# Squares of x summed by TensorE, inverse roots and half-wise scaling on GpSimd, and another order of fill and banks in the second block of a two-block transformer kernel

## The chip, the core and the metric

The kernel runs on one core of a Trainium2 chip. The engines are TensorE (PE, with its weight loads PEld), VectorE (DVE), ScalarE (ACT), GpSimd (POOL) and SyncE (SP, which issues most of the DMAs). Each engine works through its own list of instructions in order, and waits at an instruction until what that one needs is there. The metric is the device time of one execution in microseconds (us).

## The reference

Two transformer blocks run one after the other on 512 tokens of width 1024, all in float32. Cut to what matters:

```python
# first block
xn = rms_norm(x, norm_gain)            # x * rsqrt(mean(x*x, -1) + EPS) * gain
qa, ka, va, za, qi, ki, wi, qb, kb, vb, zb = split(xn @ w_in)
qa, ka, qb, kb = (rms_norm(t_per_head, its_gain) for each of the four)   # 8 heads of 64
score = sum over 4 index heads of relu(qi . ki) * wi        # causal
a_out = attention(qa, ka, va) over the 128 best keys of each token by score
b_out = dilated attention(qb, kb, vb)
x = x + concat(a_out * silu(za), b_out * silu(zb)) @ w_out
# second block
h = rms_norm(x, norm_mix)
q, (kc, vc, ks, vs, kw, vw), g_attn, u_pool, g_merge = split(h @ w_in_2)
a = (gated sum of attention on compressed, selected and windowed keys) @ w_branch_attn
b = pool_mixer(u_pool) @ w_branch_pool     # running means over 2, 4, 8, 16 tokens
x = x + (sigmoid(ga) * a + sigmoid(gb) * b) @ w_out_2
x = x + square(relu(rms_norm(x, norm_mlp) @ w_ff1)) @ w_ff2
return rms_norm(x, norm_final)
```

## The kernel before

**Products.** Every matrix product is made of three matmuls on rounded operands. A weight unit is a DMA into `wr` (or `wx`), a rounded high part `wh` (ACT, or a CAST on DVE) and a remainder `wl` (POOL as two instructions of 512 columns, or DVE as one of 1024). x is held as `XH` and `XL` in the same way, eight parts of 128 features by 512 tokens, named `xh_69` and following. The sum is wh*xh + wl*xh + wh*xl. Two `wr` tiles and three each of `wh` and `wl` take turns, so a unit's DMA waits for a remainder two units earlier. PSUM has 8 banks, by tag: three `g`, two `s`, two `pt`, one `av`. A GEMM that puts tokens on partitions (`steps_t`) takes one bank for each of four token blocks, from the tags in its argument `tags`; one that puts features there (`steps_e`) takes two `g` banks.

**Start.** Ten matmuls on a tile of zeros come first. The index GEMM (queries, keys and weights of the index heads, 324 columns) then runs in four units of two x parts each, with banks `s, s, pt, av`, and both `wh` and `wl` by DVE. `load_x` is its hook: for each part it makes `XH` (ACT), `XL` (DVE) and the squares (ACT), and POOL adds the squares of the eight parts into `ssum` (tile `th`). After the last unit `tok_stats([ssum])` sums `ssum` over the features by four matmuls of 128 x 1 against ones, and DVE makes the inverse root `rs_t`.

**First block.** The weight GEMMs run through x without its norm, and the norm is applied when a bank is read. `qk_pair(s, p)` makes queries and keys of two heads for branch b (s = "b") or a: GEMM into `raw`, squares and sums per head (`qm`), inverse roots by `rsqrt` (`qy`, with `qt` as scratch) by nine short instructions on DVE after one integer one, and one multiplication of all of `raw` by `qy`, by POOL for branch b and by DVE for branch a. PE then transposes `raw` (`pt<-ident,raw`), and ACT and DVE make the operands `qs`, `kh`, `kl`. `select` finds the 128 best keys on DVE with rounds of MAX8 and MATCH_REPLACE8, from about 69 to 162 us. The tiles `pth` and `ptl` are the two parts of transposed probabilities, `sb` the probabilities before.

**Order on the engines.** A tile scheduler sets the order outside the attention stretches. Inside them `weave` sets it by hand: it takes steps of the attention in turn and puts fill GEMMs between them, from a list that it works through in order. In the second block the first such list is taken with `prepare()`, which makes compressed keys and values; its pieces are `values_t` (values, 280 columns with the gates), `raw_t("q0")` (queries of group 0), and `pool_in(0)`, `pool_in(1)`, whose banks `evac_u` reads with DVE and then adds shifted copies on POOL, one addition for window 2 up to four for window 16 (tile `th`). `stack_group(0, ...)` transposes queries into `qs`, and `compressed(0)` uses them with compressed keys `kch`, `kcl` in a bank `s`.

Of the kernel before, what the change touches and what calls it, by code (L numbers as in the profile page):

```python
# [13 lines left out]
AF = mybir.ActivationFunctionType  # L14
OP = mybir.AluOpType
# [4 lines left out]
S = 512  # L20
# [123 lines left out]
def _program(ctx, tc, nc, ap, units, out, out1):  # L144
# [7 lines left out]
    def bank(tag):  # L152
        return ps.tile([128, 512], F32, name=tag, tag=tag, bufs={"g": 3, "s": 2, "pt": 2, "av": 1}[tag])

    def mm(o, lhsT, rhs, start, stop):
        nc.tensor.matmul(o, lhsT, rhs, start=start, stop=stop, skip_group_check=True)  # L156
# [4 lines left out]
    def act(o, i, f=AF.Copy, **kw):  # L161
        nc.scalar.activation(o, i, f, **kw)  # L162

    def stt(o, a, s, b, op0, op1, eng=None):
        (eng or nc.vector).scalar_tensor_tensor(o, a, s, b, op0=op0, op1=op1)

    def tt(o, a, b, op, eng=None):
        (eng or nc.vector).tensor_tensor(o, a, b, op=op)  # L168

    def ts(o, a, s1, s2=None, op0=OP.mult, op1=None, eng=None):  # L170
        if op1 is None:
            (eng or nc.vector).tensor_scalar(o, a, s1, None, op0=op0)
        else:
            (eng or nc.vector).tensor_scalar(o, a, s1, s2, op0=op0, op1=op1)
# [32 lines left out]
    def run(steps):  # L207
        for _ in steps:
            pass
# [7 lines left out]
    def steps_t(name, us, XH, XL, evac, tbs=range(NB), tags=("g",) * 4, hook=None, last=None, **conv):  # L217


        n = us[0][3]  # L220
        per = 512 // n if n <= 256 else 1
        tbs = list(tbs)
        groups = [tbs[q:q + per] for q in range(0, len(tbs), per)]
        banks = [bank(tags[q]) for q in range(len(groups))]
        at = lambda q, r: banks[q][:, r * n:(r + 1) * n]
        for iu, u in enumerate(us):
            then = hook and hook(u)
            k0, kk, wh, wl = wload(name, u, **conv)
            if then:
                then()  # L230
            for q, group in enumerate(groups):
                for k in range(kk):
                    for r, t in enumerate(group):
                        st = iu == 0 and k == 0 and r == 0
                        en = iu == len(us) - 1 and k == kk - 1
                        xh = XH[k0 + k][:, t * 128:(t + 1) * 128]
                        xl = XL[k0 + k][:, t * 128:(t + 1) * 128]
                        mm(at(q, r), xh, wh[:, k, :], st, False)
                        mm(at(q, r), xh, wl[:, k, :], False, False)
                        mm(at(q, r), xl, wh[:, k, :], False, en)  # L240
                    yield 3 * n * len(group)
        if last:
            last()
        for q, group in enumerate(groups):
            rest = [evac(t, at(q, r)) for r, t in enumerate(group)]
            for then in rest:
                if callable(then):
                    then()
# [18 lines left out]
        for c in range(nch):  # L267
            evac(c, banks[c])

    def rsqrt(y, m, tmp):  # L270

        ts(y.bitcast(I32), m.bitcast(I32), -0.5, 1597463007.0, OP.mult, OP.add)
        for _ in range(3):
            stt(tmp, y, -0.5, y, OP.mult, OP.mult)
            tt(tmp, tmp, m, OP.mult)
            stt(y, tmp, 1.5, y, OP.add, OP.mult)

    def weave(main, slots, fills, total):

        chain = itertools.chain(*fills)  # L280
        done = 0
        with tc.manual_schedule(engines={mybir.EngineType.PE}):
            for i in range(slots):
                next(main)
                while done < total * (i + 1) / slots:
                    c = next(chain, None)
                    if c is None:
                        break
                    done += c
            run(chain)  # L290
# [7 lines left out]
    def tok_stats(*args):  # L298
        run(tok_stats_steps(*args))

    def tok_stats_steps(parts, blocks=range(NB)):


        n = len(blocks)
        cols = slice(blocks[0], blocks[-1] + 1)
        b = bank("pt")
        for part in parts:
            for i in range(n):
                mm(b[:, i:i + 1], part[:, i * 128:(i + 1) * 128], ones, part is parts[0] and i == 0, part is parts[-1])
        m = consts.tile([128, NB], F32, name="st_m", tag="st_m")[:, :n]  # L310
        tmp = consts.tile([128, NB], F32, name="st_t", tag="st_t")[:, :n]
        y = rs_t[:, cols]
        ts(m, b[:, :n], 1.0 / D, EPS, OP.mult, OP.add)
        rsqrt(y, m, tmp)
        yield
        b = bank("pt")
        for i in range(n):
            tr(b[:, i * 128:(i + 1) * 128], y[:, i:i + 1].to_broadcast([128, 128]))
        act(rs_b[:, cols.start * 128:cols.stop * 128], b[:, :n * 128])
        yield b  # L320
# [16 lines left out]
    def T(shape, dt=F32, tag=None, bufs=1):  # L337
        return sb.tile(shape, dt, name=tag, tag=tag, bufs=bufs)

    ssum = T([128, S], tag="th")  # L340


    zero = T([128, S], F32, tag="nbm", bufs=2)
    nc.vector.memset(zero, 0.0)
# [1 line left out]
    b = bank("g")  # L346
    for _ in range(10):
        mm(b, z16[:, :128], z16[:, :512], True, True)

    def load_x(unit):  # L350
        ks = range(unit[1], unit[1] + unit[2])
        raw = {k: T([128, S], tag="mix", bufs=5) for k in ks}
        for k in ks:
            nc.sync.dma_start(raw[k], ap["xT"][:, k, :])

        def parts():
            for k, xr in raw.items():
                act(XH[k], xr, scale=ng[:, k:k + 1])
                stt(XL[k], xr, ng[:, k:k + 1], view(XH[k]), OP.mult, OP.subtract)
                if k == 0:  # L360
                    act(ssum, xr, AF.Square)
                else:
                    sq = T([128, S], tag="z", bufs=3)
                    act(sq, xr, AF.Square)
                    tt(ssum, ssum, sq, OP.add, nc.gpsimd)

        return parts

# [156 lines left out]
    def evac_idx(tb, o):  # L525
# [1 line left out]
        ts(wi[:, tb, :], idx[:, tb, 320:324], 1.0 / 16)  # L527

    gemm_t("w1", units["w1"]["idx"], XH, XL, evac_idx, hook=load_x, tags=("s", "s", "pt", "av"),
           last=lambda: tok_stats([ssum]), hi="dve", lo="dve")  # L530
    cstrip = cload("strip", [128, S], eng=nc.sync)
    gcol = cload("gcol", [128, 4], eng=nc.sync)
    gq = consts.tile([128, 2], F32, name="gq")
# [15 lines left out]
    for i in range(1, NB):  # L549
        n = (i + 1) * 128  # L550
        score[i] = T([128, n], tag=f"sel{i}")
        for h in range(4):
            b = scores(QI[h // 2][:, h % 2, i * 128:(i + 1) * 128], KIH[:, 0], KIL[:, 0], i)
            r = T([128, S], tag="sb", bufs=3)
            act(r[:, :n], b[:, :n], AF.Relu)
            prev = score[i]
            if h == 0:
                prev = T([128, S], tag="nbm", bufs=2)[:, :n]
                ts(prev, cstrip[:, (3 - i) * 128:(3 - i) * 128 + n], -1.0, eng=nc.gpsimd)
            stt(score[i], r[:, :n], wi[:, i, h:h + 1], prev, OP.mult, OP.add)  # L560

    def select(i):

# [13 lines left out]
    ML = [T([128, S], F32R, tag=f"ml{c}") for c in range(8)]  # L577
    QK, VX, Z, RAW = {}, {}, {}, {}

    def qk_pair(s, p):  # L580
        raw = T([128, NB, 4, 64], tag="raw", bufs=2)
        yield from steps_t("w1", units["w1"][f"qk{s}{p}"], XH, XL,
               lambda tb, o: act(raw[:, tb].rearrange("p h d -> p (h d)"), o, scale=rs_t[:, tb:tb + 1]))
        m = T([128, NB * 4], tag="qm", bufs=2)
        for t in range(0, NB, 2):
            sq = T([128, 2, 4, 64], tag="th")
            act(sq, raw[:, t:t + 2], AF.Square)
            nc.vector.reduce_sum(m[:, 4 * t:4 * t + 8], sq.rearrange("p b h d -> p (b h) d"), axis=AX.X)
        ts(m, m, 1.0 / 64, EPS, OP.mult, OP.add)
        y = T([128, NB * 4], tag="qy", bufs=2)  # L590
        tmp = T([128, NB * 4], tag="qt", bufs=2)
        rsqrt(y, m, tmp)
        f = raw.rearrange("p b h d -> p (b h) d")
        tt(f, f, y[:, :, None].to_broadcast([128, NB * 4, 64]), OP.mult, nc.gpsimd if s == "b" else None)
        RAW[s, p] = raw

    def stack_pair_q(s, p):
# [106 lines left out]
            for hl in range(2):  # L704
                yield pair_job(n, hl, hooks)

    run(qk_pair("b", 0))
    run(qk_pair("b", 1))
    stack_pair_q("b", 0)
    stack_pair_k("b", 0)  # L710
# [191 lines left out]
        ts(gates[:, tb], o[:, 256:280], r)  # L902

    def values_t():
        yield from steps_t("w2", units["w2"]["vv"], XH, XL, evac_v, tags=("g", "g", "g", "s"))
        act(gates, gates, AF.Tanh, scale=0.5)
        ts(gates, gates, 0.5, 0.5, OP.mult, OP.add)

# [134 lines left out]
    def pool_in(p):  # L1043
        yield from steps_e("w2", units["w2"][f"u{p}"], XH, XL, evac_u(p))
# [31 lines left out]
            yield  # L1076

    run(raw_t("kk"))
    weave(prepare(), len(order), [values_t(), raw_t("q0"), pool_in(0), pool_in(1)], 4.15 * task)
    PTH, PTL = prob_tiles(T)  # L1080
    cmp = [compressed(0), compressed(1)]
    hooks = {
# [214 lines left out]
```

## Time and profile before

| | |
|---|---|
| time, median of 3 runs | 1064.28 us (1060.01 to 1065.57) |
| the profiled execution | 1063.42 us, of which the span from first to last instruction is 1061.3 us |
| PE busy in the span | 1030.1 us, 97% |
| DVE, ACT, POOL busy | 620.3, 549.8, 318.3 us |
| mean granted TensorE clock | 0.990 of full speed |

The profile is of one execution: engine by engine, what ran when, and where an engine stood idle, which semaphore it then waited for. Times are from the span's start. A matmul's duration includes its passage through the array, and matmuls overlap, so the distance between the starts of two is what the next one costs. "[2.92 <-DVE ptl L168]" says that the engine had been idle for 2.92 us and was released by the instruction of line 168 on DVE that writes `ptl`. The 2.1 us outside the span belong to each execution.

### The profile page before, as it was taken

What the parts mean: (1) busy time and instruction counts of PE and PEld (TensorE: products, weight loads), DVE (VectorE), ACT (ScalarE), POOL (GpSimd) and SP (SyncE); (2) the same over time, 40 slices, a digit from 0 to 9 for tenths busy, and PEclk for the clock granted to TensorE, in tenths of its full rate; (3) what the DMA queues carried; (4) which work ended last, traced back from release to release, by engine and by line L of the source; (5) the groups of instructions that cost most, each with busy time, mean ns of one, the idle gap of its engine ahead of it and who ended that gap; (6) DMA issues with size and microseconds to landing.
All of it is one profiled execution on the core that took longest, in us unless ns stands there. A gap on an engine that the chain in (4) does not pass through costs nothing.

```text
span 1061.3 us, 15516 instructions
## 1 busy us (share of the span) xinstructions
PE 1030.1 (97%) x5675; PEld 886.7 (84%) x5675; DVE 620.3 (58%) x1388; ACT 549.8 (52%) x1041; POOL 318.3 (30%) x280
## 2 busy tenths in 40 slices
PE   7999999999999999899999999999999999999996
PEld 5998988999888897787888888888888888888886
DVE  6589998766757755867867323545442234443333
ACT  4557676787765354678788433434331123443321
POOL 5543442455645337522222467400000000000001
PEclk8999999999999999999999999999999999999999
DMA  5334433444567364111111223522222223222212
GB/s 186 107 96 139 117 107 100 137 125 124 164 204 233 125 200 139 60 40 41 61 53 48 70 90 114 184 80 99 100 99 88 91 99 100 99 99 87 92 60 80
DMA packets 41835, 115.07 MB, mean 108 GB/s; under 512 B 5904, under 2 KB 7312, under 8 KB 41760
## 3 DMA queue, kind: packets, MB, share of 16 engines
q1 hardware_dynamic: 41568, 113.96, 33.4%
q8 instruction: 45, 0.74, 0.3%
q14 instruction: 30, 0.25, 0.1%
q0 software_dynamic: 192, 0.12, 0.1%
HBM read 97.90 MB, written 6.33 MB: 98 GB/s over the span
## 4 chain that ended last, share of the span: by engine, by line
PE 78%; DVE 13%; ACT 3%; DMA 2%; issue 2%; POOL 1%; SPq 1%; DVEq 0%; ACTq 0%; POOLq 0%
PE g L156 66%; PE s L156 4%; PE av L156 4%; PE pt L159 4%; DVE sel L568 1%; DVE m L567 1%; DVE ptl L168 1%; DMA wx<-in_w_dram 1%; DVE sb L399 1%; ACT wh L162 1%; POOL wl L168 1%; DVE mix L168 1%; DVE raw L168 1%; PE pt L156 1%; DMA mix<-in_xT_dram 1%
## 5 line engine op out<-in xcount | busy, mean ns | idle before, releaser
L168 POOL TENSOR_TENSOR wl<-wr,wh 128x512 fp32r<-128x512 f32 (+1 forms) x148 | 194.5, 1335 | 233.9 <-ACT wh L162 220.7
L162 ACT ACTIVATE wh<-wr 128x1024 fp32r<-128x1024 f32 (+1 forms) x124 | 130.3, 1052 | 171.8 <-PE g L156 141.8
L156 PE MATMUL g<-wh,xh 128*128 128x256 f32 (+1 forms) x504 | 147.2, 292 | 1.1 <-ACT raw L162 1.1
L156 PE MATMUL g<-wl,xh 128*128 128x256 f32 (+1 forms) x504 | 143.8, 285 | 1.9 <-POOL wl L168 1.9
L156 PE MATMUL g<-wh,xl 128*128 128x256 f32 (+1 forms) x504 | 143.2, 284 | 0.0
L168 DVE TENSOR_TENSOR wl<-wr,wh 128x1024 fp32r<-128x1024 f32 (+1 forms) x54 | 66.7, 1235 | 102.5 <-ACT wh L162 102.4
L156 PE MATMUL g<-xh,wh 128*128 128x512 f32 x304 | 125.2, 413 | 0.0
L156 PE MATMUL g<-xh,wl 128*128 128x512 f32 x304 | 119.8, 395 | 0.0
L156 PE MATMUL g<-xl,wh 128*128 128x512 f32 x304 | 119.7, 394 | 0.0
L168 POOL TENSOR_TENSOR res<-res,rs_b 128x256 f32<-128x256 f32 x6 | 4.2, 732 | 366.2 <-ACT rs_b L162 366.2
L156 PE MATMUL g<-hh,wl 128*128 128x512 f32 (+1 forms) x272 | 103.4, 380 | 0.0
L156 PE MATMUL g<-hl,wh 128*128 128x512 f32 (+1 forms) x272 | 103.0, 379 | 0.0
L156 PE MATMUL g<-hh,wh 128*128 128x512 f32 (+1 forms) x272 | 102.2, 376 | 0.0
L156 PE MATMUL g<-yh,wl 128*128 128x512 f32 x256 | 100.9, 394 | 0.0
L156 PE MATMUL g<-yl,wh 128*128 128x512 f32 x256 | 100.3, 392 | 0.0
L156 PE MATMUL g<-yh,wh 128*128 128x512 f32 x256 | 99.7, 389 | 0.0
L156 PEld LDWEIGHTS g<-wl,xh 128*128 128x128 f32 x504 | 96.4, 191 | 3.7 <-POOL wl L168 2.3
L156 PEld LDWEIGHTS g<-wh,xh 128*128 128x128 f32 x504 | 96.3, 191 | 2.4 <-ACT raw L162 1.3
L156 PEld LDWEIGHTS g<-wh,xl 128*128 128x128 f32 x504 | 96.3, 191 | 0.7 <-issue 0.5
L162 ACT ACTIVATE sb<-sb,mx 128x512 f32<-128x512 f32 (+3 forms) x128 | 71.5, 559 | 33.7 <-DVE mx L399 32.4
L162 ACT ACTIVATE sb<-sb,ri 128x512 f32<-128x512 f32 (+3 forms) x128 | 70.8, 558 | 34.2 <-DVE ri L404 25.8
L162 ACT ACTIVATE wh<-wx 128x1024 fp32r<-128x1024 f32 x35 | 37.1, 1060 | 86.1 <-PE g L156 73.3
(275 smaller groups left out, 2263.0 us busy)
## 6 DMA issues: line engine op xcount, KB each, us to landing
wr<-in_w_dram SPq DMA_DIRECT2D x48, 512.0 KB, 3.7
wr<-in_wf_dram SPq DMA_DIRECT2D x43, 512.0 KB, 3.2
wx<-in_wf_dram SPq DMA_DIRECT2D x21, 512.0 KB, 3.2
wr<-in_wo_dram SPq DMA_DIRECT2D x15, 512.0 KB, 3.6
wx<-in_w_dram SPq DMA_DIRECT2D x12, 512.0 KB, 3.2
mix<-in_xT_dram SPq DMA_DIRECT2D x16, 256.0 KB, 3.9
strip<-vec_dram SPq DMA_DIRECT2D x16, 256.0 KB, 3.3
x_dram<-mix SPq DMA_DIRECT2D x16, 256.0 KB, 3.5
```

Source lines behind the costliest of these rows:

```text
L156: nc.tensor.matmul(o, lhsT, rhs, start=start, stop=stop, skip_group_check=True)
L159: nc.tensor.transpose(o, in_, ident[:n, :n])
L162: nc.scalar.activation(o, i, f, **kw)
L168: (eng or nc.vector).tensor_tensor(o, a, b, op=op)
L399: nc.vector.tensor_tensor_reduce(out=p[:, :n], in0=b[:, :n], in1=nbm, scale=1.0, scalar=3e38, op0=OP.add, op1=OP.min, accum_out=mx)
L567: nc.vector.max(out=m8, in_=w)
L568: nc.vector.match_replace(out=w, in_to_replace=m8, in_values=w, imm_value=-3e38)
```

## The change

1. `x_stats`, a generator that `load_x` feeds, sums the squares of each part on TensorE: four matmuls 128 x 1 against ones per part into one bank `pt`, 32 in all in place of 4. The tile `ssum` and POOL's seven additions are gone; the inverse root follows the eighth part.
2. The first score term of `select`'s input uses the mask strip itself with a subtraction; three POOL instructions (`nbm<-strip`) are gone.
3. `rsqrt` can run its three rounds on another engine. All qk pairs but (b, 0) run them on POOL, four instructions of 128 x 16 a round, 12 in place of DVE's 9; the integer step stays on DVE. The multiplication of `raw` is made in two halves, queries first. For (b, 0) the `wl` and the scaling are now on DVE.
4. In the second block the list of fill pieces begins with `pool_in(1)`, and `values_t` uses banks `g, s, g, g` in place of `g, g, g, s`.

```diff
+    def rsqrt(y, m, tmp, eng=None):
         ts(y.bitcast(I32), m.bitcast(I32), -0.5, 1597463007.0, OP.mult, OP.add)
+        if eng:
+            for _ in range(3):
+                tt(tmp, y, y, OP.mult, eng)
+                tt(tmp, tmp, m, OP.mult, eng)
+                ts(tmp, tmp, -0.5, 1.5, OP.mult, OP.add, eng)
+                tt(y, y, tmp, OP.mult, eng)
+            return
         for _ in range(3):
             stt(tmp, y, -0.5, y, OP.mult, OP.mult)
...
-    ssum = T([128, S], tag="th")
...
+    def x_stats():
+        b = bank("pt")
+        while True:
+            part, k = yield
+            for i in range(NB):
+                mm(b[:, i:i + 1], part[:, i * 128:(i + 1) * 128], ones, k == i == 0, k == KD - 1)
+            if k == KD - 1:
+                run(tok_stats_steps(None, bank_done=b))
...
-                if k == 0:
-                    act(ssum, xr, AF.Square)
-                else:
-                    sq = T([128, S], tag="z", bufs=3)
-                    act(sq, xr, AF.Square)
-                    tt(ssum, ssum, sq, OP.add, nc.gpsimd)
+                sq = T([128, S], tag="z", bufs=3)
+                act(sq, xr, AF.Square)
+                stats.send((sq, k))
...
     gemm_t("w1", units["w1"]["idx"], XH, XL, evac_idx, hook=load_x, tags=("s", "s", "pt", "av"),
-           last=lambda: tok_stats([ssum]), hi="dve", lo="dve")
+           hi="dve", lo="dve")
...
             if h == 0:
-                prev = T([128, S], tag="nbm", bufs=2)[:, :n]
-                ts(prev, cstrip[:, (3 - i) * 128:(3 - i) * 128 + n], -1.0, eng=nc.gpsimd)
-            stt(score[i], r[:, :n], wi[:, i, h:h + 1], prev, OP.mult, OP.add)
+                stt(score[i], r[:, :n], wi[:, i, h:h + 1], cstrip[:, (3 - i) * 128:(3 - i) * 128 + n],
+                    OP.mult, OP.subtract)
...
-        rsqrt(y, m, tmp)
-        f = raw.rearrange("p b h d -> p (b h) d")
-        tt(f, f, y[:, :, None].to_broadcast([128, NB * 4, 64]), OP.mult, nc.gpsimd if s == "b" else None)
+        pool = nc.gpsimd if (s, p) != ("b", 0) else None
+        rsqrt(y, m, tmp, pool)
+        y = y.rearrange("p (b h) -> p b h", h=4)
+        for x in (slice(0, 2), slice(2, 4)):
+            tt(raw[:, :, x], raw[:, :, x], y[:, :, x, None].to_broadcast([128, NB, 2, 64]), OP.mult,
+               pool if s == "b" else None)
...
-    run(qk_pair("b", 0))
+    run(qk_pair("b", 0, "dve"))
...
-        yield from steps_t("w2", units["w2"]["vv"], XH, XL, evac_v, tags=("g", "g", "g", "s"))
+        yield from steps_t("w2", units["w2"]["vv"], XH, XL, evac_v, tags=("g", "s", "g", "g"))
...
-    weave(prepare(), len(order), [values_t(), raw_t("q0"), pool_in(0), pool_in(1)], 4.15 * task)
+    weave(prepare(), len(order), [pool_in(1), values_t(), raw_t("q0"), pool_in(0)], 4.15 * task)
```

**PE at the start.** The last of the ten matmuls on zeros (`g<-nbm`) and the first rows of the index GEMM, before:

```order
L156 MATMUL g<-nbm 128x512
L156 MATMUL s<-wh,xh_69 128x324 x2
L156 MATMUL pt<-wh,xh_69 128x324
L156 MATMUL av<-wh,xh_69 128x324
L156 MATMUL s<-wl,xh_69 128x324
```

and after:

```order
L156 MATMUL g<-nbm 128x512
L156 MATMUL pt<-ones,z 128x1 x8
L156 MATMUL s<-wh,xh_69 128x324 x2
L156 MATMUL pt<-wh,xh_69 128x324
L156 MATMUL av<-wh,xh_69 128x324
L156 MATMUL s<-wl,xh_69 128x324
```

Eight matmuls on the squares (`z`) of two parts now stand ahead of the unit's GEMM, and eight more ahead of each later unit; the four on the summed squares behind the last unit are gone.

**POOL in the first block.** Remainders of weights (`wl`) and the scaling of the second to fourth pair of branch b, before:

```order
L168 TENSOR_TENSOR wl<-wr,wh 128x512 x3
L168 TENSOR_TENSOR raw<-raw,qy 128x1024
L168 TENSOR_TENSOR wl<-wr,wh 128x512 x7
L168 TENSOR_TENSOR raw<-raw,qy 128x1024
L168 TENSOR_TENSOR wl<-wr,wh 128x512 x8
L168 TENSOR_TENSOR raw<-raw,qy 128x1024
```

and after, from the remainders ahead of the second pair's scaling on:

```order
L168 TENSOR_TENSOR wl<-wr,wh 128x512 x10
L168 TENSOR_TENSOR qt<-qy 128x16
L168 TENSOR_TENSOR qt<-qt,qm 128x16
L174 TENSOR_SCALAR qt<-qt 128x16
L168 TENSOR_TENSOR qy<-qy,qt 128x16
L168 TENSOR_TENSOR qt<-qy 128x16
L168 TENSOR_TENSOR qt<-qt,qm 128x16
L174 TENSOR_SCALAR qt<-qt 128x16
L168 TENSOR_TENSOR qy<-qy,qt 128x16
L168 TENSOR_TENSOR qt<-qy 128x16
L168 TENSOR_TENSOR qt<-qt,qm 128x16
L174 TENSOR_SCALAR qt<-qt 128x16
```

The twelfth short row (`qy<-qy,qt`), the two halves of `raw` and six rows of `wl` follow. The short rows stand where before one long multiplication stood, with the weights' remainders of later units queued behind them.

**ACT in the second block.** Queries of group 0 (`qs`), the pooled branch's input (`mh` with a number) and compressed values (`vc`), before:

```order
L162 ACTIVATE mh_5212<-th 128x512
L162 ACTIVATE qs<-pt 64x512 x2
L162 ACTIVATE wh<-wr 128x1024
L162 ACTIVATE qs<-pt 64x512 x2
L162 ACTIVATE mh_5229<-th 128x512
```

and after:

```order
L162 ACTIVATE wh<-wr 128x1024
L162 ACTIVATE qs<-pt 64x512 x2
L162 ACTIVATE wh<-wr 128x1024
L162 ACTIVATE qs<-pt 64x512 x2
L162 ACTIVATE vc<-pt,half 128x2x64 x4
L162 ACTIVATE wh<-wx 128x1024
L162 ACTIVATE mh_5401<-th 128x512
```

Both query rows now stand ahead of the `mh` of `pool_in(0)`; the `mh` rows of `pool_in(1)` have moved further up, ahead of the compressed keys.

## Rows read from the trace of the kernel before

**Rows 1.** The page, part 1: busy us, share of the span, instructions.

```profile
PE 1030.1 (97%) x5675; PEld 886.7 (84%) x5675; DVE 620.3 (58%) x1388; ACT 549.8 (52%) x1041; POOL 318.3 (30%) x280
```

**Rows 2.** What PE waited for, whole span: total us, times, longest.

```profile
PE s L156 <- DVE wh L197: 3.9, 3, 2.0
PE pt L159 <- DVE ptl L168: 3.4, 2, 2.9
...
PE s L156 <- DVE qs L165: 1.9, 1, 1.9
...
PE av L156 <- ACT pch L162: 1.5, 1, 1.5
```

**Rows 3.** Busy time by stretch; granted clock, DMA share, GB/s last.

```profile
77.00:165.00 88.00, 82.96 (x586) 76.91 (x585) 85.40 (x257) 57.98 (x129) 35.52 (x27) 0.98 0.42 120
...
365.00:375.00 10.00, 7.49 (x46) 7.03 (x46) 5.63 (x9) 5.20 (x9) 4.11 (x4) 0.83 0.34 91
...
418.00:430.00 12.00, 9.96 (x43) 7.75 (x42) 10.05 (x14) 4.66 (x8) 7.60 (x11) 0.86 0.26 87
430.00:500.00 70.00, 65.36 (x384) 55.81 (x383) 51.92 (x165) 55.40 (x130) 24.09 (x25) 1.00 0.13 46
```

**Rows 4.** Timeline of PE at the start: start, duration, instruction.

```profile
1.50 4.45 PE L156 MATMUL g<-nbm 128*128 128x512 bf16 x10 [1.50 <-DVE nbm L344]
...
27.45 0.31 PE L156 MATMUL s<-wl,xh 128*128 128x324 f32 x1
...
27.60 0.31 PE L156 MATMUL s<-wh,xl 128*128 128x324 f32 x1
...
30.41 0.95 PE L156 MATMUL pt<-ones,th 128*128 128x1 f32 x8
...
31.21 0.36 PE L156 MATMUL g<-wh,xh 128*128 128x256 f32 x1
```

**Rows 5.** Timeline of POOL and DVE at the start.

```profile
14.13 4.80 POOL L168 TENSOR_TENSOR th<-th,z 128x512 f32<-128x512 f32 x3
...
17.74 1.55 DVE L197 CAST wh<-wr 128x648 fp32r<-128x648 f32 x1
...
21.70 0.48 DVE L197 CAST wh<-wr 128x648 fp32r<-128x648 f32 x1
```

**Rows 6.** Busy time and granted clock of short stretches after PE stood idle.

```profile
21.17:26.73 5.56, 5.56 (x20) 5.56 (x21) 2.42 (x4) 1.06 (x1) 0.90 (x1) 0.50 0.58 190
160.47:163.49 3.02, 3.02 (x8) 2.45 (x9) 2.20 (x10) 1.05 (x2) 0.00 (x0) 0.50 0.54 130
...
422.00:426.00 4.00, 3.84 (x12) 2.96 (x13) 3.87 (x6) 1.55 (x3) 3.35 (x4) 0.62 0.06 25
```

**Rows 7.** Groups of DVE instructions between 77 and 160 us.

```profile
L165 DVE SCALAR_TENSOR_TENSOR qt<-qy 128x16 f32<-128x16 f32 x7 | 3.1, 438 | 0.0
...
L168 DVE TENSOR_TENSOR qt<-qt,qm 128x16 f32<-128x16 f32 x7 | 2.7, 390 | 0.0
...
L165 DVE SCALAR_TENSOR_TENSOR qy<-qt,qy 128x16 f32<-128x16 f32 x7 | 2.6, 376 | 0.0
...
L174 DVE TENSOR_SCALAR qm<-qm 128x16 f32<-128x16 f32 x2 | 0.3, 166 | 0.0
```

**Rows 8.** Groups of POOL instructions by shape, whole span.

```profile
L168 POOL TENSOR_TENSOR nbm<-strip,sel 128x512 f32<-128x512 f32 x8 | 10.4, 1296 | 6.4 <-DVE mx L399 5.0 <-DMA strip<-vec_dram 1.4
...
L168 POOL TENSOR_TENSOR nbm<-strip,sel 128x256 f32<-128x256 f32 x8 | 6.7, 842 | 7.3 <-DVE qt L165 4.1 <-DVE mx L399 3.2
...
L1011 POOL MEMSET th<- 128x16 f32 x10 | 1.1, 111 | 4.6 <-DVE ml L168 3.4 <-DVE th L168 1.0
```

**Rows 9.** Timeline at the third pair's scaling.

```profile
110.79 1.91 POOL L168 TENSOR_TENSOR raw<-raw,qy 128x1024 f32<-128x1024 f32 x1 [2.07 <-DVE qy L165]
...
112.84 0.60 PE L159 MATMUL pt<-ident,raw 128*128 128x128 f32 x4
```

**Rows 10.** Timeline of ACT at group 0's queries, second block.

```profile
419.56 0.63 ACT L162 ACTIVATE mh<-th 128x512 fp32r<-128x512 f32 x1 [3.13 <-DVE th L168]
```

More of the change, by code (lines that the diff above doesn't have):

```diff
@@ L268, in steps_e @@
             evac(c, banks[c])
-    def rsqrt(y, m, tmp):
+    def rsqrt(y, m, tmp, eng=None):
         ts(y.bitcast(I32), m.bitcast(I32), -0.5, 1597463007.0, OP.mult, OP.add)
+        if eng:
[5 more added lines that the diff above has]
+            return
         for _ in range(3):
@@ L299, in tok_stats, with tok_stats_steps @@
         run(tok_stats_steps(*args))
-    def tok_stats_steps(parts, blocks=range(NB)):
+    def tok_stats_steps(parts, blocks=range(NB), bank_done=None):
         n = len(blocks)
         cols = slice(blocks[0], blocks[-1] + 1)
-        b = bank("pt")
-        for part in parts:
+        b = bank_done or bank("pt")
+        for part in parts or ():
             for i in range(n):
@@ L348, in _program @@
         mm(b, z16[:, :128], z16[:, :512], True, True)
+    def x_stats():
[6 more added lines that the diff above has]
+                run(tok_stats_steps(None, bank_done=b))
+    stats = x_stats()
+    next(stats)
     def load_x(unit):
@@ L555, in _program @@
             act(r[:, :n], b[:, :n], AF.Relu)
-            prev = score[i]
             if h == 0:
-                prev = T([128, S], tag="nbm", bufs=2)[:, :n]
-                ts(prev, cstrip[:, (3 - i) * 128:(3 - i) * 128 + n], -1.0, eng=nc.gpsimd)
-            stt(score[i], r[:, :n], wi[:, i, h:h + 1], prev, OP.mult, OP.add)
+                stt(score[i], r[:, :n], wi[:, i, h:h + 1], cstrip[:, (3 - i) * 128:(3 - i) * 128 + n],
+                    OP.mult, OP.subtract)
+            else:
+                stt(score[i], r[:, :n], wi[:, i, h:h + 1], score[i], OP.mult, OP.add)
     def select(i):
@@ L578, in _program, with qk_pair @@
     QK, VX, Z, RAW = {}, {}, {}, {}
-    def qk_pair(s, p):
+    def qk_pair(s, p, lo="pool"):
         raw = T([128, NB, 4, 64], tag="raw", bufs=2)
         yield from steps_t("w1", units["w1"][f"qk{s}{p}"], XH, XL,
-               lambda tb, o: act(raw[:, tb].rearrange("p h d -> p (h d)"), o, scale=rs_t[:, tb:tb + 1]))
+               lambda tb, o: act(raw[:, tb].rearrange("p h d -> p (h d)"), o, scale=rs_t[:, tb:tb + 1]), lo=lo)
         m = T([128, NB * 4], tag="qm", bufs=2)
```

## The prediction

> **What bounds the kernel now.** The page comes first, and in it the busy time of the engines: PE works 1030.1 of 1061.3 us [rows 1], so only two things can shorten the kernel: less work on PE, or fewer of the 31 us in which it stands idle. The change adds matmuls, so its gain can lie in the idle time alone. The waits of PE say what released it [rows 2]: nearly all releases come from DVE, in three kinds: weights at the start (`wh`, 3.9 us), transposed probabilities (`ptl` 3.4), queries (`qs` 1.9). The table of stretches then says where [rows 3]: 5.0 us idle in 77 to 165, where DVE is busy 85.4 of 88 us; 2.5 us in 365 to 375; 2.0 in 418 to 430; 4.6 in 430 to 500. A stall costs more than its length: in short stretches behind idle time the granted clock is 0.50 (the 1.2 GHz level) or near it [rows 6]. So I add to each stall what the slow stretch behind it loses, its length times one minus the granted clock.
>
> The sum is made on the profiled 1063.42 us, 2.1 of which lie outside the span. That is 0.86 under the median of the runs, so the result is raised by as much.
>
> **Squares on TensorE.** Added: 28 matmuls of 128 x 1. The trace has four of them as eight records in 30.41 to 31.21, so 0.20 us each [rows 4], and 32 cost 6.4 us, 5.6 more than now. Removed: nothing that PE did, but seven POOL additions, three of which fill 4.80 us from 14.13 [rows 5], and POOL's three strip instructions. What they did is seen on DVE: the CAST of a weight unit took 1.55 us beside one and 0.48 alone [rows 5], and PE waited 3.9 us for `wh` [rows 2]. After the last wait 5.56 us passed at 0.50, so 2.8 were lost to the clock [rows 6]. If DVE stays ahead, the index GEMM runs without a hole: matmuls start 0.15 us apart (27.45, 27.60) [rows 4], a unit has 24 of them, so 3.55 us, with 1.6 us of squares ahead of it. Four units are 20.6 us; PE is done with the zeros at 1.50 + 4.45 = 5.95, so the first `g` matmul starts at about 26.6 in place of 31.21 [rows 4]. That is 4.6 us gained. Bounds: 6 if the short matmuls cost a quarter less, 2 if one wait of 2.0, the longest for `wh` [rows 2], and some slow clock remain. The first unit's squares fill PE while weights are awaited, and the holes were longer than the added work.
>
> **Inverse roots and halves.** DVE loses nine instructions per pair; between 77 and 160 the 21 of them in three groups take 3.1 + 2.7 + 2.6 = 8.4 us [rows 7]. DVE is the engine that PE waits for there, 5.0 us idle [rows 3] and 3.02 us at 0.50 behind the longest stall [rows 6], 1.5 lost: 6.5 in all. The stalls add up over a chain on DVE that is nearly always busy, so 8.4 us off it could clear all of them. What works against it: the remainder and scaling of pair (b, 0) move to DVE ahead of this stretch, and the new POOL instructions slow DVE. By the CAST, which took 1.07 us longer beside an addition of 4.80 / 3 = 1.60 [rows 5], POOL's time costs DVE up to two thirds of it; 28 instructions at the 0.25 chosen below make 7 us, so 4.7 of the 8.4 may come back. I take 4 of the 6.5, with bounds of 0 and 6.5.
>
> What POOL pays: 12 instructions of 128 x 16 per pair. The trace has none but a MEMSET of that shape, 0.111 us; the line through 128 x 512 (1.296) and 128 x 256 (0.842) gives 0.42 at 16 columns; the outer bound is 0.84 itself [rows 8]. I take 0.25, about the middle of the first two, so 3.0 us a chain where DVE's nine, at the means of their groups, take 3 x (0.438 + 0.390 + 0.376) = 3.6 [rows 7]. The halves add up to the old 1.91 [rows 9], queries ready after the first. Behind the chain POOL queues the next units' `wl`, which PE needs. In the new order the scaling of the second and third pair stands one weight unit earlier, two instructions of 128 x 512 or 2.6 us [rows 8], so the third, whose `raw` ended at 112.70 and was read at 112.84 [rows 9], isn't later than now.
>
> A rule speaks against this part. The Trainium skill, GPSIMD Engine Reference, section 4.1 (Engine selection), puts elementwise work on VectorE and calls GpSimd about half as fast with two inputs. Applied to DVE's mean of 0.40 it gives, as an estimate, 0.80 an instruction and, put into the third rival's formula below, about 1078; applied to DVE's undisturbed 0.166 [rows 7] it gives 0.33 and leaves the sum as it is. Rows of such an instruction on POOL don't exist here, so the trace doesn't decide; the MEMSET and the slope speak for the lower end.
>
> **Second block.** At 419.56 ACT rounds `mh` of the pooled branch, 0.63 us and 3.13 us late, ahead of the queries [rows 10], and PE waits 1.9 for DVE's `qs` behind it [rows 2]; then 4.00 us pass at 0.62, 1.5 lost [rows 6]. In the new order both `qs` stand ahead of that `mh`, and `pool_in(1)`, which brings POOL seven additions, has been worked off some 30 us before. I take 2.8 of the 3.4. Later, the attention's start loses 4.6 us between 430 and 500 [rows 3], 1.5 of it for `pch` [rows 2], while `pool_in(1)`'s additions hold POOL and DVE; with these gone I take 1.8. The stall at 365 to 375, 2.5 us idle and 1.7 of clock (0.83 over 10 us) [rows 3], stands mostly ahead of the fill list's first bank; I take 1 of it. Sum: 5.6, bounds 0 and 9. Costs against it: `values_t`'s fourth bank is now a `g` that `pool_in(1)`'s second column block held; DVE frees it behind a `wl` and POOL's additions, a wait of up to 2.5 (the idle at 365 to 375 is the nearest row) with 1.5 of clock. I don't expect it whole, since ACT and DVE idle there.
>
> **Sum.** 4.6 + 4 + 5.6 = 14.2: 1063.4 - 14.2 = 1049.2 for the profiled execution, 1050 as a median.
>
> **Rivals.**
> - *The second block only moves its stall.* The fourth bank takes 2.5 + 1.5 of the 5.6. Then 1054 to 1057. For it: the bank is freed by DVE behind three POOL additions; against: nothing else wants DVE there.
> - *Only the start pays.* DVE's relief is given back by waits for POOL's chains, and the fill order is neutral: 1064.3 - 4.6 = 1059.7, or 1062 with the start's low bound. For it: every pair now crosses to POOL and back; against: DVE busy 85.4 of 88 us there [rows 3].
> - *GpSimd's short instructions are dear* (the other side). A chain and scaling then take 12c + 1.9 against 3.6 + 1.9 now, less a head start of 2.6: at c = 0.84 [rows 8] each `raw` is 12c - 6.2 = 3.9 us late, over seven pairs 27 us, and the `wl` queued behind it are late too: 1064.3 - 10.2 + 27 = 1081, where 10.2 is the gain at the start and in the second block. It becomes a loss where 7 x (12c - 6.2) passes 10.2, so from c = 0.64. For it: the shortest two-input row here is 0.842 and none is smaller in shape; against: the MEMSET's 0.111 and the slope between the shapes.
> - *More than forecast.* All stalls named vanish: 6 + 6.5 + 9 = 21.5, so 1043, or less if fewer slow stretches follow.
>
> **How the numbers follow.** Forecast (1045 to 1054) 0.52; second block moves its stall (1054 to 1057.5) 0.21; only the start pays (1057.5 to 1063) 0.13; more than forecast (1038 to 1045) 0.08; dear GpSimd (above 1063) 0.06. The range 1041 to 1061 leaves out the last, half of the one before and the upper part of the third. Half a per cent is 5.3 us, about what a measurement of this kernel tells from no change: below 1059.0 counts as faster, above 1069.6 as slower. Faster 0.80, same 0.14, slower 0.06, by these cases, the third split at 1059 and the last mostly above 1069.6.
>
> **What would show it.** Right: the first `g` matmul near 26.6, PE without waits for `wh` and `wl` ahead of it; 128 x 16 on POOL near 0.25; no wait for `ptl` near 157; no `qs` wait near 419 less the shift. Wrong: PE released by POOL's `raw` at several pairs; a wait of PE on a `g` bank in `values_t`, followed by a clock near 0.5; squares late, so that PE waits for ACT at the start.

## The result, and the profile after

| | before | after |
|---|---|---|
| median of 6 runs | 1065.03 us (1060.01 to 1066.13) | 1056.73 us (1055.27 to 1058.85) |
| ratio of the runs | | 0.9926, 95% interval 0.991 to 0.9943 |
| profiled execution | 1063.42 us, span 1061.3 | 1058.85 us, span 1057.0 |

The change saves 8.3 us by the medians and 0.74% (0.57 to 0.90) by the ratio of the runs, which is 7.9 us: faster, inside the range given, but 6.7 us above the predicted time. Timed once more, the same kernel had a ratio of 0.9949 (0.9936 to 0.9962), 5.4 us. The time lies in the rival case in which the second block only moves its stall (1054 to 1057.5). The profiled execution is the longest of the six.

The page's busy times say that PE is now busy for 1.3 us more than in [rows 1], in a span 4.3 us shorter:

```profile
PE 1031.4 (98%) x5731; PEld 891.1 (84%) x5731; DVE 601.0 (57%) x1333; ACT 550.6 (52%) x1041; POOL 319.1 (30%) x352
```

What PE waited for after the change, as in [rows 2] (total us, times, longest):

```profile
PE g L156 <- DVE th L168: 6.4, 1, 6.4
PE pt L159 <- DVE ptl L168: 4.0, 4, 1.5
...
PE s L156 <- DVE wh L197: 1.1, 1, 1.1
...
PE g L156 <- POOL wl L168: 1.0, 2, 0.7
PE g L156 <- ACT raw L162: 0.8, 1, 0.8
```

The waits for `qs` of 1.9 and `pch` of 1.5 are gone, `wh` fell from 3.9 to 1.1, and the longest wait for `ptl` from 2.9 to 1.5. One wait is new and longer than any single one before: 6.4 us for a `g` bank that DVE frees by `th`. The stretches after the change, against [rows 3] and [rows 6] (busy us by engine, granted clock, DMA share, GB/s):

```profile
8.06:11.41 3.35, 3.35 (x11) 3.05 (x12) 3.35 (x6) 3.09 (x6) 0.00 (x0) 0.50 0.92 294
...
75.00:163.00 88.00, 85.25 (x609) 79.66 (x609) 83.21 (x253) 62.15 (x137) 46.72 (x68) 1.00 0.43 122
...
372.00:396.00 24.00, 16.86 (x101) 15.75 (x100) 11.98 (x17) 8.36 (x12) 14.71 (x20) 0.79 0.58 169
...
387.67:392.00 4.33, 4.33 (x18) 4.33 (x19) 1.74 (x3) 1.30 (x2) 2.13 (x4) 0.50 0.32 118
...
414.00:430.00 16.00, 15.72 (x83) 12.81 (x82) 9.02 (x21) 6.97 (x15) 6.93 (x6) 1.00 0.33 117
430.00:500.00 70.00, 67.67 (x404) 58.32 (x403) 51.06 (x169) 57.79 (x136) 20.23 (x18) 1.00 0.13 46
```

PE's idle time in the first block's stretch fell from 5.0 to 2.8 us, at a granted clock of 1.00. Around the queries it fell from 2.0 to 0.3, in 430 to 500 from 4.6 to 2.3. The stretch 372 to 396 has 7.1 us idle. PE works at the 1.2 GHz level (granted clock 0.50) in two stretches now, 8.06 to 11.41 behind a wait for the first `wh`, and 387.67 to 392 behind the new wait. The timeline of PE at the start, against [rows 4]:

```profile
5.16 1.84 PE L156 MATMUL pt<-ones,z 128*128 128x1 f32 x16
8.06 0.88 PE L156 MATMUL s<-wh,xh 128*128 128x324 f32 x2 [1.06 <-DVE wh L197]
...
13.35 1.84 PE L156 MATMUL pt<-ones,z 128*128 128x1 f32 x16
15.05 0.40 PE L156 MATMUL s<-wh,xh 128*128 128x324 f32 x1
...
29.33 0.28 PE L156 MATMUL g<-wh,xh 128*128 128x256 f32 x1
```

The squares stand where the order put them; eight matmuls take 1.70 us (13.35 to 15.05). Every unit but the first runs without a hole. The first `g` matmul starts at 29.33, not at 26.6.

POOL's groups by shape now hold the instructions that no row of before had, against [rows 8]:

```profile
L168 POOL TENSOR_TENSOR raw<-raw,qy 128x512 f32<-128x512 f32 x6 | 6.6, 1125 | 0.2
L168 POOL TENSOR_TENSOR qy<-qy,qt 128x16 f32<-128x16 f32 x21 | 5.1, 243 | 1.5
L168 POOL TENSOR_TENSOR qt<-qy 128x16 f32<-128x16 f32 x21 | 4.7, 226 | 12.0 <-DVE qy L174 10.9
L168 POOL TENSOR_TENSOR qt<-qt,qm 128x16 f32<-128x16 f32 x21 | 4.7, 225 | 1.6
L174 POOL TENSOR_SCALAR qt<-qt 128x16 f32<-128x16 f32 x21 | 4.3, 202 | 1.8
```

A chain is 3 x (0.226 + 0.225 + 0.202 + 0.243) = 2.7 us; 3.0 was taken. The two halves are 2.25 us in place of 1.91.

Last, what stood ahead of the `th` for which PE waited, from the timeline of the second block:

```profile
377.05 0.33 SPq L191 DMA_DIRECT2D wr<-in_cw_dram  x1
...
380.11 2.34 POOL L168 TENSOR_TENSOR wl<-wr,wh 128x280 fp32r<-128x280 f32 x2
...
382.45 1.03 POOL L168 TENSOR_TENSOR th<-th 128x512 f32<-128x512 f32 x1
...
384.17 1.06 ACT L162 ACTIVATE wh<-wr 128x1024 fp32r<-128x1024 f32 x1 [5.29 <-DMA wr<-in_cw_dram]
...
385.26 1.23 DVE L168 TENSOR_TENSOR wl<-wr,wh 128x1024 fp32r<-128x1024 f32 x1 [4.04 <-ACT wh L162]
...
386.93 0.69 DVE L168 TENSOR_TENSOR th<-g,rs_b 128x512 f32<-128x512 f32 x1
...
387.67 0.60 PE L156 MATMUL g<-wh,xh 128*128 128x280 f32 x1 [6.41 <-DVE th L168]
```

`in_cw` holds the weights of the compressed keys. Their DMA is issued at 377.05, and ACT can round them at 384.17. DVE, whose list has their remainder ahead of the second `th`, stands idle for 4.04 us until then. POOL's third window sum, which `th` also stands behind, ends at 383.48, itself behind a `wl` of `values_t`. PE had been idle since 381.26. Behind that sum alone `th` could have started near 383.7 and PE near 384.5, so of the 6.41 us some 3.2 go to POOL's sums and some 3.2 to the late remainder, an estimate from these rows.

### The profile page after: what moved, and what is told of

Its sections match the earlier page's. It is cut to its first block, busy times and chain, and to the rows that moved or that the text cites. A ratio compares the mean times of both kernels' runs of the same rounds, so it can differ in the third digit from the quotient of the medians.

```text
span 1057.0 us, 15626 instructions
## 1 busy us (share of the span) xinstructions
PE 1031.4 (98%) x5731; PEld 891.1 (84%) x5731; DVE 601.0 (57%) x1333; ACT 550.6 (52%) x1041; POOL 319.1 (30%) x352
## 4 chain that ended last, share of the span: by engine, by line
PE 90%; DVE 6%; ACT 2%; DMA 1%; issue 1%; POOL 0%; SPq 0%; DVEq 0%; ACTq 0%
PE g L156 74%; PE s L156 5%; PE av L156 4%; PE pt L159 4%; PE pt L156 1%; DMA wr<-in_cw_dram 1%; DVE ptl L168 1%; DVE raw L168 1%; DMA wr<-in_w_dram 1%; DVE sb L414 0%; DVE sel L583 0%; ACT raw L162 0%; DVE mix L168 0%; DVE m L582 0%; ACT sb L162 0%
## 5 line engine op out<-in xcount | busy, mean ns | idle before, releaser
L162 ACT ACTIVATE wh<-wx 128x1024 fp32r<-128x1024 f32 (+1 forms) x35 | 36.7, 1048 | 80.1 <-PE g L156 75.2
```

## The experiments

Each was timed in five rounds against the kernel before on the same chip; that one's medians were 1064.78 us for the first four, 1064.19 for the next four, 1063.05 for three and 1063.9 for the last. These four groups ran on four chips, so the ratio to the kernel before, and not the time, compares an experiment with one of another group. "The first g" is the start of the first `g` matmul of the first block.

**The order and banks alone.**

```diff
-[values_t(), raw_t("q0"), pool_in(0), pool_in(1)]
+[pool_in(1), values_t(), raw_t("q0"), pool_in(0)]
...
-tags=("g", "g", "g", "s"))
+tags=("g", "s", "g", "g"))
```

> The kernel before with the new order of the fill list and the new banks of values_t alone. Theory A (what the second block gave back: PE waits 6.4 us in values_t for a g bank and runs at a granted clock of 0.50 for 4.3 us behind it, which outweighs the 2.7 and 2.2 us gained at 400-430 and 430-500): 1064 to 1068 us, with a wait of 5 to 7 us of PE g on DVE th. Theory B (the second block gains as forecast, and the missing 6 us were lost at the start and in the first block): 1058 to 1061 us.

Measured: 1061.02 us, ratio 0.9982 (0.9961 to 1.0004). The time lies between the two, and neither number held. The wait is there, shorter:

```profile
387.86 0.40 PE L156 MATMUL g<-wh,xh 128*128 128x280 f32 x1 [4.51 <-DVE th L168]
```

By the interval the part gains 4 us at most, not 5.6 (1.9 by the ratio, 3.8 by the medians), and it loses nothing that can be measured.

**Inverse roots, halves and the first pair alone**: part 3 of the change on the kernel before.

```diff
-        rsqrt(y, m, tmp)
+        rsqrt(y, m, tmp, pool)
...
-    run(qk_pair("b", 0))
+    run(qk_pair("b", 0, "dve"))
```

> The kernel before with the inverse roots on GpSimd, the scaling in halves and the first pair's remainder on VectorE alone. Theory A (the first block pays about 4 us, as in the sum): 1060 to 1062 us, the 2.9 us wait for ptl near 157 gone or halved. Rival (the chains on GpSimd only move the waits, and the 4 us came with the shifted start): 1064 to 1066 us.

Measured: 1059.95 us, ratio 0.9969 (0.9953 to 0.9985), 3.3 us (4.8 by the medians). The longest wait for `ptl` fell from 2.9 to 1.5 us. That is theory A's range, but for 0.05 us.

**Remainders of `values_t` on VectorE**, in the changed kernel.

```diff
-tags=("g", "s", "g", "g"))
+tags=("g", "s", "g", "g"), lo="dve")
```

> The changed kernel with the remainders of the weights of values_t made by VectorE in place of GpSimd. Theory A (GpSimd's additions for pool_in(1) hold up these remainders, so the wr tile comes free late, so the next weights' DMA, their high part and VectorE's remainder are late, and the th behind them that frees the bank): the 6.4 us wait falls to 0 to 2 us and the time to 1048 to 1052 us. Theory C (the bank is late by itself, since VectorE waits for GpSimd's additions that stand ahead of th): the wait stays at 4 us or more, 1055 to 1058 us.

Measured: 1051.85 us, ratio 0.9896 (0.9875 to 0.9917), better than both kernels. The wait for `th` is 0.9 us:

```profile
383.89 0.39 PE L156 MATMUL g<-wh,xh 128*128 128x280 f32 x1 [0.94 <-DVE th L168]
```

So the new wait cost 3.2 to 5.6 us, by the changed kernel's two ratios. The edit does two things, though: POOL's sums come earlier, and in the new order the second `th` stands ahead of the late remainder, whose weights are ready at 384.00 here and at 384.17 in the changed kernel, each on its own clock:

```profile
383.15 0.69 DVE L168 TENSOR_TENSOR th<-g,rs_b 128x512 f32<-128x512 f32 x1
...
384.00 1.06 ACT L162 ACTIVATE wh<-wr 128x1024 fp32r<-128x1024 f32 x1 [2.90 <-DMA wr<-in_cw_dram]
...
385.09 1.22 DVE L168 TENSOR_TENSOR wl<-wr,wh 128x1024 fp32r<-128x1024 f32 x1 [0.46 <-ACT wh L162]
```

The last experiment takes `th` out from behind both.

**The change without its order and banks**, that is the first experiment's edit the other way round on the changed kernel.

> The changed kernel with the fill list and the banks of before. Theory A (the order lost 6.4 us and gained 4.9): 1053 to 1056 us, no wait over 2 us in 360-400, and the waits near 419 and 437 to 450 back. Theory B (the order gains as forecast): 1061 to 1063 us.

Measured: 1058.49 us, ratio 0.995 (0.9931 to 0.997); the changed kernel had 0.9926 and 0.9949. So the order and banks gave the changed kernel 0 to 2.6 us. The waits for `qs` (1.7) and `pch` (1.5) came back, the one for `th` went: theory A's rows, though the time is 2.5 us above what it gave. All nine runs (1055.52 to 1060.14) lie below theory B's 1061 to 1063.

**Squares on TensorE and the strip alone**: parts 1 and 2 of the change on the kernel before.

```diff
-                    tt(ssum, ssum, sq, OP.add, nc.gpsimd)
+                stats.send((sq, k))
```

> The kernel before with the squares on TensorE and the strip used directly, alone. Theory S (the 5.6 us of short matmuls eat what the stalls at the start gave back; the forecast's 31.21 us for the first g matmul was a late one of a start that varies): 1062 to 1065 us, the first g matmul between 28.5 and 31. Rival (the part gives the 4.6 us of the sum, and the profiles seen had late weights): 1059 to 1061 us.

Measured: 1064.62 us, ratio 1.0009 (0.9993 to 1.0025): nothing. The first g was at 29.72. What it might have saved is also spent at the second pair, where PE waited 2.8 us for POOL's `raw`, 1.1 in the kernel before: in the profiles the first g comes 1.5 us sooner than in the kernel before, but the first matmul on `mh`, in the first block's output GEMM, 2.0 later (289.07 for 287.10). What the strip is worth was not tested by itself.

**Squares on GpSimd again**, in the kernel with the remainders of `values_t` on VectorE: the edit above the other way round.

> The changed kernel with the remainders of values_t on VectorE, and the squares summed by GpSimd as before. Theory S: 1051 to 1054 us, as with squares on TensorE (1051.85), waits for wh and wl back at the start, no more than 1 us slower. Rival: 1056 to 1057 us, 4.6 us slower.

Measured: 1051.05 us, ratio 0.9882 (0.9856 to 0.9908), against 0.9896 with squares on TensorE. The first g was at 29.01, with waits of 2.6 us each for `wh` and `wl`. The difference lies within the intervals. Theory S, from both sides.

**More matmuls on zeros**, in the kernel with the remainders of `values_t` on VectorE.

```diff
-    for _ in range(10):
+    for _ in range(15):
```

> The changed kernel with the remainders of values_t on VectorE and 15 in place of 10 matmuls on zeros at the start. If the start is slow because PE waits for the first weights and then runs at the 1.2 GHz level (8.06 to 11.41 us in the changed kernel's profile), work up to the weights' arrival gives 0.5 to 1.5 us: 1050 to 1051.5 us, first g matmul at 28.5 to 29.5. If the level depends on something else, as in the run where matmuls stood 0.27 us apart up to 14.0 us without a wait, it costs the zeros' 1 to 2 us: 1052 to 1054 us.

Measured: 1050.38 us, ratio 0.987 (0.9841 to 0.9899), the fastest of all; the intervals of this, of 0.9896 and of 0.9882 (squares on GpSimd, ten matmuls on zeros) overlap. The first g was at 28.28, and from the zeros on no wait of PE stood ahead of it:

```profile
1.49 5.26 PE L156 MATMUL g<-nbm 128*128 128x512 bf16 x15 [1.49 <-DVE nbm L349]
6.59 1.84 PE L156 MATMUL pt<-ones,z 128*128 128x1 f32 x16
...
28.28 0.29 PE L156 MATMUL g<-wh,xh 128*128 128x256 f32 x1
```

**Inverse roots back on VectorE**, same base; the halves stay.

```diff
-        rsqrt(y, m, tmp, pool)
+        rsqrt(y, m, tmp)
```

> The changed kernel with the remainders of values_t on VectorE, and the three rounds of the inverse roots back on VectorE; the halves stay. Theory A (the relief of VectorE by the chains is what the first block gains): 1055 to 1057 us, 3 to 5 slower than with GpSimd (1051.85), the ptl wait near 155 longer than 2 us. Rival (the earlier scaling by halves and the first pair on VectorE made the gain): 1051 to 1053 us.

Measured: 1056.99 us, ratio 0.993 (0.9902 to 0.9957), against 0.9896 (0.9875 to 0.9917) with GpSimd's chains: 3.6 us more by the ratios, 5.1 by the medians. The time lies in theory A's range by the median. The longest `ptl` wait was 1.7 us, less than expected, but PE waited 1.9 us for POOL's `raw`, which no run with the chains on GpSimd did. In 77 to 165 PE was idle 4.9 us, where the base had 2.7 in the same stretch of its work:

```profile
77.00:165.00 88.00, 83.07 (x596) 77.55 (x595) 85.84 (x278) 59.27 (x133) 38.15 (x32) 1.00 0.42 119
...
340.00:356.00 16.00, 14.94 (x75) 12.35 (x74) 10.27 (x21) 5.72 (x9) 7.67 (x14) 0.89 0.56 187
```

The two profiled executions start alike (first g at 31.01 and 30.98). Up to the first matmul on `mh` this one falls 2.4 us behind, and 3.1 more by the transposes of the second inverse root, where PE waits 1.1 for `ssum` and runs at a low granted clock behind it (second row); nothing shows that to come from the chains. So the chains are worth some 2.4 us in the first block, and the halves alone don't make the gain.

The other profiles tell the same: from the first g to the first matmul on `mh` the ten profiled executions with the chains on GpSimd took 250.7 to 252.0 us, and the four without took 255.9 (before), 254.8 (order alone), 259.4 (squares alone) and 254.2 (this one).

**Zeros and squares on GpSimd**: 15 matmuls on zeros, remainders of `values_t` on VectorE, squares as before.

> Remainders of values_t on VectorE and 15 matmuls on zeros, with the squares summed by GpSimd as before. If GpSimd's additions cost what the sum says (VectorE's work on weights slowed beside them, PE waiting for wh and wl), the first g matmul comes at 29 to 31 us and the time is 1051.5 to 1054 us, 1 to 3 over the same with squares on TensorE (1050.38). If the additions cost nothing once PE is kept at work up to the first weights: 1046 to 1049 us, first g matmul near 25.

Measured: 1052.79 us, ratio 0.9903 (0.9888 to 0.9918), 2.4 us more than with squares on TensorE by the medians and 3.5 by the ratios, whose intervals still overlap a little. The first g was at 30.19, 1.9 us later, with PE waiting 3.1 us for `wl` and 1.7 for `wh`; at the first matmul on `mh` 0.8 of that is left (280.93 for 280.10). So with PE at work up to the first weights the squares on TensorE seem to pay. Against the squares on GpSimd with ten matmuls on zeros, 1051.05 us, the best kernel with them on TensorE gains 0.7 us, which the intervals don't tell from nothing.

**Zeros and the old banks**: `values_t` on `g, g, g, s` in the kernel with 15 matmuls.

> Remainders of values_t on VectorE, 15 matmuls on zeros, pool_in(1) first, but values_t with the banks g, g, g, s of before. Theory A (a third g bank is free only after pool_in(1)'s second th, whichever token block takes it): the wait for th moves to the third token block, so it comes earlier and is 1 to 2.5 us in place of 0.9: 1050.5 to 1052.5 us. Rival (the order of banks does nothing): 1050 to 1050.7 us, the wait under 1 us.

Measured: 1052.25 us, ratio 0.9896 (0.9883 to 0.991), with a wait of 2.1 us for `th` in place of 0.9. The intervals of the two ratios overlap, but the wait moved as theory A said: a third `g` bank is what is scarce, and the new order of banks asks for it later.

**The changed kernel once more.**

> The changed kernel once more, on the chip of these runs: 1055 to 1058 us, with the 6.4 us wait for th in the second block, and the first g matmul between 28.5 and 31.

Measured: 1057.25 us, ratio 0.9949 (0.9936 to 0.9962), a wait of 5.1 us for `th`, the first g at 29.41.

**Both banks read first.** `evac_u` copies both banks into `th`, of which there is a fourth tile now, then sums; weights and their remainders keep their places in the changed kernel.

```diff
-            tt(u[:, 16:], o, rs_b, OP.mult)
-            cur = u
...
+            tt(us[g][:, 16:], o, rs_b, OP.mult)
+            if c:
+                window(g - 1)
+                window(g)
```

> The changed kernel in which evac_u reads both banks of pool_in into th before either is summed over windows (with a fourth th tile); weights, their remainders and their places on the engines as in the changed kernel. Theory D (the wait of 5 to 6.4 us is the place of the second th on VectorE alone: behind the first window sums of GpSimd and behind the remainder of compressed-key weights that land late): no wait for th above 0.5 us in 372 to 392, granted clock there 1.00, time 1049.5 to 1052 us. Theory A (GpSimd's late remainders of values_t and the late weights behind them hold PE as well): a wait of 2 us or more on wl or wh takes its place, 1053 to 1056 us.

Measured: 1054.01 us (1049.92 to 1055.07), ratio 0.9903 (0.9877 to 0.9929). The profiled execution is the fastest of the six, at 1049.92. In it the wait for `th` is gone, and the granted clock in 372 to 392 is 1.00. A shorter wait stands a little further on, for the late remainder itself:

```profile
372.00:392.00 20.00, 17.53 (x129) 16.45 (x128) 14.63 (x18) 10.67 (x16) 16.70 (x21) 1.00 0.72 208
...
383.99 0.39 PE L156 MATMUL s<-wl,qs 128*128 128x256 f32 x1 [1.64 <-DVE wl L168]
```

So most of the 6.4 us and the slow clock behind it came from the place of one short copy on DVE. The compressed keys' weights, late by themselves, are worth 1.6 us here: theory D with a remainder of theory A. This execution owes part of its time to an early first g, 27.31. But its stretch from the transposes of the second inverse root to the first matmul on `pch` doesn't depend on that: 91.4 us, where the changed kernel's two profiles have 97.4 and 95.1 and the kernel with `values_t`'s remainders on VectorE 90.2. The median lies in A's band; by the ratios the edit gains 2.4 to 4.9 us on the changed kernel's 0.9926 and 0.9949.

## Why the prediction was right, and which terms were off

**Stage by stage.** The starts of the same matmuls in the profiles, in us, say where the gain arose (second profile: the repeat of the changed kernel):

| from the one before, up to | before | after | second profile | gained | forecast |
|---|---|---|---|---|---|
| first g | 31.21 | 29.33 | 29.41 | 1.9, 1.8 | 4.6 |
| first matmul on `mh`, end of the first block's attention | 287.10 | 281.13 | 281.17 | 4.1, 4.1 | 4 |
| transposes of the second inverse root (`pt<-ident,rs_t`) | 353.39 | 347.42 | 348.06 | 0.0, -0.6 | 0 |
| first matmul on `pch` | 449.69 | 444.86 | 443.16 | -1.1, 1.2 | 5.6, with the next |
| last matmul | 1053.62 | 1049.10 | 1047.46 | -0.3, -0.4 | |

```profile
287.10 0.39 PE L156 MATMUL g<-mh,wh 128*128 128x512 f32 x1
353.39 0.60 PE L159 MATMUL pt<-ident,rs_t 128*128 128x128 f32 x4
449.69 0.50 PE L156 MATMUL av<-pch,vc 128*128 128x512 f32 x1 [1.46 <-ACT pch L162]
...
281.13 0.39 PE L156 MATMUL g<-mh,wh 128*128 128x512 f32 x1
347.42 0.60 PE L159 MATMUL pt<-ident,rs_t 128*128 128x128 f32 x4
444.86 0.49 PE L156 MATMUL av<-pch,vc 128*128 128x512 f32 x1
```

The first three rows are of the kernel before, the others of the changed one. So one term of three came as forecast, and two fell short. The time lies in the range because that reaches 11 us above the predicted 1050; it does not bear these two terms out.

**Where it was right.** The first block was forecast at 4 and gave 3.3 us alone by the ratio and 4.1 in the profiles, of which the chains by themselves make 2.4; the profiles before and after show 2.3 us less idle time and the 1.5 us behind the longest stall. The price that decided the opposite rival, c = 0.25 taken and a loss from 0.64, measured 0.20 to 0.24. So the head start was enough, and no wait of PE for POOL's `raw` is left. The Trainium skill, GPSIMD Engine Reference, section 4.1 (Engine selection), calls GpSimd about half as fast with two inputs. Here such a row takes 0.225 to 0.243 us, where VectorE's undisturbed row of that size took 0.166 with one input [rows 7] and 0.164 with two (`t<-th,icnt`, profile after), so the trace is milder at this size; and since VectorE was the engine with a queue, where the same rows had means of 0.376 to 0.438 [rows 7], its relief counted for more than the price. The terms for the queries and for 430 to 500 were also met: 2.8 forecast for the first, 3.3 read (1.8 us idle and 1.5 of clock); 1.8 and 2.3 for the second. One reading was too strong: by the page of waits DVE released 15.7 of PE's 23.1 us, not nearly all.

**The second block, 5.6 forecast.** The failed step is "I don't expect it whole, since ACT and DVE idle there", on the price of the fourth bank. It came with 2.5 us of waiting as its bound and cost 6.4, or 5.1 in the repeat, plus 2.2 of slow clock in the first of these. The prediction named what stands ahead of the `th`, a `wl` and POOL's additions, and so had the mechanism, also as its first rival; it did not work out when each of them can run, and took the bound from the idle time of another stretch. DVE was idle indeed, but idle in front of an instruction that it could not pass: the remainder of weights that land late, and POOL's sums, each for about half of the wait by the estimate above. The last experiment and the one with `values_t`'s remainders on VectorE show it. Alone the part gave 1.9 us, and at most 4; in the changed kernel it gave nothing that the profiles agree on.

**The start, 4.6 forecast.** The failed step is the comparison of 26.6 with 31.21. The work was sized nearly right: 1.70 us of squares a unit for 1.6. But 31.21 was a late case of a start that varies from one execution to the next: the kernels with squares on GpSimd and ten matmuls on zeros had their first g at 31.21, 27.88, 29.24 and 29.01, mean 29.3; those with squares on TensorE and ten at 29.33, 30.98, 28.70, 29.72, 31.01, 29.41 and 27.31, mean 29.5. And 26.6 took for granted that PE runs at the higher level from 5.95 on. In the profile after, it waits for the first `wh` and goes at 0.50 from 8.06 to 11.41. That is most of the 2.7 us between 26.6 and 29.33. By the two means the 1.9 us won against 31.21 in these two profiles are luck. The contention was real: the CAST takes 0.49 to 0.50 us in all four units now, 1.55 beside POOL's additions before [rows 5]. The Trainium skill, GPSIMD Engine Reference, section 8 (Key points), which says that VectorE and GpSimd share SBUF interfaces and contend when VectorE's instruction uses two ports or has two SBUF inputs, agrees with it, though no run shows which ports the CAST used. But the added matmuls, 6.0 us by the measured 1.70 a unit less the 0.80 of before, eat up what its end gives. With more work on zeros ahead the squares on TensorE are 2.4 us better than on GpSimd by the medians, and 0.7 better than the best with them on GpSimd.

**What stays open.** By their ratios on 1064 us the parts alone sum to -1.0 + 3.3 + 1.9 = 4.2 us, and the changed kernel's two ratios stand for 7.9 and 5.4. By the medians the parts sum to -0.4 + 4.8 + 3.8 = 8.2, and the changed kernel has 8.3 and 5.8. So whether the parts help each other is not settled. Why the start sometimes stays slow for long (below) was not settled either, nor why the compressed keys' weights took 7.1 us from their issue to their rounding in the changed kernel.

## What to carry to other kernels

An idle engine is no cover for a step in its list: read from the order what stands ahead of the step and work out when the latest of it can run, above all a remainder of weights that a DMA brings. Where one engine has a queue and another has air, short work moved to the slower engine can pay, as it did here at 0.20 to 0.24 us for an instruction that takes 0.164 undisturbed. Measure a stage that varies from one execution to the next in several profiles before a gain is worked out from one of them.

## What the runs showed of the hardware

In two executions (remainders of `values_t` on VectorE, and the same with the inverse roots back on VectorE) TensorE went at about half its pace from the start of the squares up to 14.0 us, without a wait ahead. In the first of them sixteen records of squares took 3.41 us in place of 1.84, and index matmuls stood 0.27 us apart in place of 0.15, then 0.15 from 14.27 on. That spacing of 0.27 is the one that the changed kernel's profile has between 8.73 and 10.89, where the granted clock is 0.50, the 1.2 GHz level. Here its column shows 1.00:

```profile
5.74 3.41 PE L156 MATMUL pt<-ones,z 128*128 128x1 f32 x16
...
10.24 0.47 PE L156 MATMUL s<-wl,xh 128*128 128x324 f32 x1
10.51 0.47 PE L156 MATMUL s<-wh,xl 128*128 128x324 f32 x1
...
14.27 0.31 PE L156 MATMUL av<-wl,xh 128*128 128x324 f32 x1
14.41 0.31 PE L156 MATMUL av<-wh,xl 128*128 128x324 f32 x1
```

The stretches of the same execution:

```profile
10.00:14.00 4.00, 4.00 (x16) 4.00 (x16) 3.27 (x7) 2.38 (x5) 0.00 (x0) 1.00 0.96 299
16.00:30.90 14.90, 14.90 (x112) 14.90 (x112) 5.64 (x17) 4.48 (x7) 0.00 (x0) 1.00 0.42 138
```

In 10 to 14 us 16 matmuls ran in 4.00 us, so in this stretch the spacing of the matmuls told the pace and the column did not. Whether the clock was low there or something else held the matmuls (the DMA engines were busy for 0.96 of it) is not shown. The first g of the two executions came at 30.98 and 31.01, the latest of those with squares on TensorE, though PE never waited behind the zeros.
